# Delta rule's triangular inverse: its transpose is brought forward by products, the inverse is taken from it by TensorE transposes

## The chip, the cores and the metric

The kernel runs on one core of one Trainium2 chip, in one launch. The metric is the device time of that launch in microseconds (us), and lower is better. TensorE (PE) does the matrix products and transposes, VectorE (DVE) and ScalarE (ACT) move results out of PSUM, GpSimd (POOL) does a few small things, and SyncE (SP) issues the transfers.

## The reference, cut to what matters

Two transformer-like blocks run over 1024 tokens of width 1024. The first holds a gated delta rule (4 heads of 128) beside a dilated attention (8 heads of 64), then a projection and a gated feed-forward layer; the second is dense work. Only the delta rule is touched. For each chunk of tokens and each head it solves a unit lower triangular system:

```
lmat = dec_strict * kk * bc[..., None, :]
rhs = jnp.concatenate([vc, gam * kc], axis=-1)
sol = lax.linalg.triangular_solve(lmat, rhs, left_side=True, lower=True, unit_diagonal=True)
u_v, w_k = sol[..., :Dv], sol[..., Dv:]
```

The kernel uses chunks of 128 tokens, so there are 8 chunks, each with four 128x128 systems.

## The kernel before, in words

`gdn_intra` (L881) works on one chunk c for four heads at once; every tile is 128x512, four 128x128 blocks side by side, and each step is a group of four instructions on PE. It forms the strictly triangular matrix LT, and then builds the inverse U and its transpose T by doubling blocks: seven levels, the first of which is elementwise. Two PSUM tiles, pT and pU, hold the running T and U. Each level lv from 1 to 6 does this:

- PE: four products LT x T into a fresh PSUM tile (named ps_G in the profile).
- DVE: this tile times a mask of the level, into G in SBUF.
- PE: four products that add U x G to pT (ps_T), and four that add G x U to pU (ps_pU). At level 6 only pU is needed.
- ACT: copies pT to T and pU to U (at level 6 only U).

Ahead of the loop, pT is filled by four transposes of U, and pU by four transposes of T. After the loop U feeds `w` and the sequential part (`gdn`: ps_u, ps_S from fp32, ps_o). Matrix products of the delta rule are in fp32: the trace shows a weight load and a matmul twice for each product, and once for each transpose. Products run through `mm` (L281), transposes through `tp` (L291) and `tpacc` (L296, which leaves the rest of the PSUM bank as it is), ACT copies through `act` (L311), DVE products through `tt` (L315).

The order of the instructions on each engine is set when the program is built. `Weaver.run` (L137) holds many tasks as Python generators, with estimated costs, picks the next one by estimated readiness and priority, and emits its instructions up to the next `yield`. So the PE queue weaves the chunks' chains with work that does not depend on them: the in-projections of the attention (ps_dil, ps_dv) and, for each attention head, the scores whose maximum is looked for (`dil_scan`: ps_S and ps_S8 from arR, read by DVE). Two neighbouring chunks are in flight at a time: chunk c+1 starts when chunk c has passed level 1 (`ghalf`). `evac` (L343) spawns a copy out of PSUM as a task of its own. When the last scan's maxima are known, they go through DRAM to all heads, and then the attention proper starts (`dil_pv`: ps_T from arR and ps_O). PSUM has eight tiles of 128x512, handed out in turn by `psum` (L357). Engines take their instructions in the order emitted.

Of the kernel before, what the change touches and what calls it, by code (L numbers as in the profile page):

```python
# [73 lines left out]
def after(*evs):  # L74
    def cond():
        return max((e.t for e in evs), default=0.0) if all(e.done for e in evs) else -1.0
    return cond
# [181 lines left out]
class Prog(Weaver):  # L259
# [621 lines left out]
    def gdn_intra(self, c, t):  # L881
        gs = self.gs
        K, Q, V, X, KEM, AT, LT, U, T, GKM = t
        E = KEM
        HH = range(GH)
        for dst, src in ((K, self.kf), (Q, self.qf), (V, self.vf)):
            self.dma(dst, src[:, c * P:(c + 1) * P].rearrange("(h p) t -> p h t", p=P), 262144)
        yield "PE"
        pG = self.ps4("gcb")
        for h in HH:  # L890
            self.tpacc(pG[:, h], gs["gc"][:, c, h:h + 1].to_broadcast([P, P]), h == 0)
        pR = self.ps4("rkb")
        for h in HH:
            self.tp(pR[:, h], gs["rkc"][:, c, h:h + 1].to_broadcast([P, P]))
        pk = self.ps4("kt")
        for h in HH:
            self.tp(pk[:, h], K[:, h])
        pv = self.ps4("vt")
        for h in HH:
            self.tp(pv[:, h], V[:, h])  # L900
        self.tt(X, K, pR, ALU.mult)
        self.act(T, pG, AF.Exp)
        nx = self.ready("PE")
        self.act(V, pv)
        if c:
            for h in HH:
                self.act(GKM[:, h], pk[:, h], AF.Copy, scale=gs["gk"][:, c, h:h + 1])
        self.at = nx
        yield "PE"
        mk = self.maskb  # L910
        for h in HH:
            self.mm(pG[:, h], self.identb, mk, False, True, True)
        pA = self.ps4("A")
        for h in HH:
            self.mm(pA[:, h], K[:, h], Q[:, h], True, True)
        pL = self.ps4("L")
        for h in HH:
            self.mm(pL[:, h], K[:, h], X[:, h], True, True)
        for h in HH:
            self.act(E[:, h], pG[:, h], AF.Exp, bias=gs["ngc"][:, c, h:h + 1])  # L920
        for h in HH:
            self.act(E[:, h], E[:, h], AF.Copy, scale=gs["brk"][:, c, h:h + 1])
        if c:
            self.tt(Q, Q, T, ALU.mult)
        self.tt(LT, pL, E, ALU.mult)
        self.tt(K, LT, self.matb(self.lvl[0]), ALU.mult)
        self.tt(U, self.matb(self.ident), K, ALU.subtract)
        nx = self.ready("PE")
        self.tt(AT, pA, E, ALU.mult)
        for h in HH:  # L930
            self.act(KEM[:, h], pk[:, h], AF.Copy, scale=gs["ke"][:, c, h:h + 1])
        self.at = nx
        yield "PE"
        pT = self.ps4("T")
        for h in HH:
            self.tpacc(pT[:, h], U[:, h], h == 0)
        self.act(T, pT)
        yield "PE"
        pU = self.ps4("pU")
        for h in HH:  # L940
            self.tpacc(pU[:, h], T[:, h], h == 0)
        G = X
        for lv in range(1, 7):
            pG1 = self.ps4("G")
            for h in HH:
                self.mm(pG1[:, h], LT[:, h], T[:, h], True, True)
            self.tt(G, pG1, self.matb(self.lvl[lv]), ALU.mult)
            yield "PE"
            if lv == int(self.STAG):
                self.ghalf[c].set(self.ready())  # L950
            if lv < 6:
                for h in HH:
                    self.mm(pT[:, h], U[:, h], G[:, h], False, True, True)
            for h in HH:
                self.mm(pU[:, h], G[:, h], U[:, h], False, True, True)
            if lv < 6:
                self.act(T, pT)
                nx = self.ready("PE")
                self.act(U, pU)
                self.at = nx  # L960
            else:
                self.act(U, pU)
            yield "PE"
        if c:
            pw = self.ps4("w")
            for h in HH:
                self.mm(pw[:, h], GKM[:, h], U[:, h], True, True)
            self.act(LT, pw)
        self.intra[c] = (Q, AT, KEM, LT, U, V)
# [1146 lines left out]
```

## Time and profile before

| | us |
|---|---|
| median of 3 runs | 2616.55 (2616.05 to 2617.04) |
| the profiled execution, its own time | 2619.11 |
| span of the profiled execution | 2617.3 |
| PE busy | 2540.3 (97%) |
| DVE busy | 1370.7 (52%) |
| ACT busy | 807.9 (31%) |

The span is what the profiler saw from the first to the last instruction. Busy is the union of an engine's instructions, so an engine that is busy all the time has nothing left to hide behind. Matmuls overlap with each other, so the duration of one says less than the distance between the starts of two groups.

### The profile page before, as it was taken

How to read it: one execution, taken by the hardware profiler on the slowest of the kernel's cores; microseconds unless marked ns; L12 is line 12 of the kernel's file. 1: busy time of each engine (PE TensorE's matmuls, PEld its weight loads, DVE VectorE, ACT ScalarE, POOL GpSimd, SP SyncE). 2: the span in 40 equal slices, each digit the busy share in tenths (PEclk: the TensorE clock that was granted, in tenths of full speed). 3: DMA queues.
4: the chain of work that ended last, by engine and by line, in shares of the span. 5: the costliest groups of instructions: out<-in, count | busy, mean ns of one | idle time of the engine just before them, and what ended most of it. 6: DMA issues, size and time to landing. Idle time of an engine off the chain costs nothing.

```text
span 2617.3 us, 31361 instructions
## 1 busy us (share of the span) xinstructions
PE 2540.3 (97%) x13001; PEld 2180.4 (83%) x13001; DVE 1370.7 (52%) x1868; ACT 807.9 (31%) x1306; POOL 121.1 (5%) x245
## 2 busy tenths in 40 slices
PE   7999999988989999999999999989999999999998
PEld 6888999988978888888888888877788888888887
DVE  5441343454654555555555567969554444444444
ACT  5322443453541422222222235253232121212122
POOL 1010000000000000000000001050000000000000
PEclk9999999998989999999999999999999999999999
DMA  5232222232441111111111113102211111111111
GB/s 189 71 104 85 84 67 62 80 80 69 106 130 57 41 49 49 49 50 50 49 50 49 50 66 101 61 9 90 71 41 57 41 57 41 57 41 57 41 49 65
DMA packets 175164, 170.80 MB, mean 65 GB/s; under 512 B 25985, under 2 KB 148254, under 8 KB 175022
## 3 DMA queue, kind: packets, MB, share of 16 engines
q1 hardware_dynamic: 175022, 168.80, 21.2%
q8 instruction: 102, 1.67, 0.3%
q14 instruction: 40, 0.33, 0.0%
HBM read 145.50 MB, written 23.23 MB: 64 GB/s over the span
## 4 chain that ended last, share of the span: by engine, by line
PE 61%; issue 28%; DVE 4%; ACT 3%; DMA 2%; POOL 2%; SPq 0%; POOLq 0%; ACTq 0%; DVEq 0%
PE ps_up L281 18%; PE ps_dn L281 9%; PE ps_in L281 5%; PE ps_out L281 5%; PE ps_vg L281 3%; PE ps_dil L281 3%; PE ps_T L281 2%; ACT arF L311 2%; PE ps_S L281 2%; PE ps_z L281 2%; PE ps_O L281 2%; PE ps_dv L281 2%; DVE arF L327 2%; PE ps_pU L281 1%; PE ps_G L281 1%
## 5 line engine op out<-in xcount | busy, mean ns | idle before, releaser
L281 PE MATMUL ps_up<-arR 128*128 128x512 f32 x3648 | 831.5, 389 | 0.0
L281 PEld LDWEIGHTS ps_up<-arR 128*128 128x128 f32 x3648 | 684.5, 188 | 142.1
L315 DVE TENSOR_TENSOR arR<-arF,arR 128x1024 fp32r<-128x1024 f32 (+3 forms) x283 | 347.6, 1236 | 610.0 <-ACT arR L311 609.5
L281 PE MATMUL ps_dn<-arR 128*128 128x512 f32 x2592 | 591.8, 389 | 0.0
L311 ACT ACTIVATE arR<-arF 128x1024 fp32r<-128x1024 f32 (+3 forms) x297 | 311.2, 1071 | 852.3 <-PE ps_dn L281 394.3
L281 PEld LDWEIGHTS ps_dn<-arR 128*128 128x128 f32 x2592 | 486.4, 188 | 101.0
L315 DVE TENSOR_TENSOR arF<-arF,ps_dn 128x512 f32<-128x512 f32 x416 | 279.6, 684 | 183.2 <-PE ps_dn L281 183.2
L327 DVE SCALAR_TENSOR_TENSOR arF<-arF,pcol 128x1024 f32<-128x1024 f32 (+1 forms) x276 | 311.4, 1149 | 22.5 <-ACT arF L311 17.5
L311 ACT ACTIVATE arF<-arF 128x1024 f32<-128x1024 f32 (+3 forms) x158 | 134.8, 860 | 272.5 <-DVE arF L315 138.5
L281 PE MATMUL ps_out<-arR 128*128 128x512 f32 x768 | 182.2, 398 | 2.7 <-DVE arR L315 2.7
L281 PEld LDWEIGHTS ps_out<-arR 128*128 128x128 f32 x768 | 146.7, 192 | 34.4 <-DVE arR L315 3.7
L311 ACT ACTIVATE arF<-ps_up 128x512 f32<-128x512 f32 x152 | 89.5, 589 | 187.0 <-PE ps_up L281 187.0
L281 PE MATMUL ps_in<-arR 128*128 128x512 f32 x576 | 137.7, 399 | 0.0
L281 PEld LDWEIGHTS ps_in<-arR 128*128 128x128 f32 x576 | 109.4, 192 | 23.9
L315 DVE TENSOR_TENSOR arF<-arF 128x1024 f32<-128x1024 f32 (+4 forms) x91 | 89.1, 979 | 28.8 <-ACT arF L311 14.8
L281 PE MATMUL ps_dil<-arR 128*128 128x512 f32 x384 | 97.4, 403 | 0.0
L281 PE MATMUL ps_vg<-arR 128*128 128x512 f32 x384 | 88.3, 390 | 0.0
L281 PEld LDWEIGHTS ps_vg<-arR 128*128 128x128 f32 x384 | 71.8, 188 | 14.8
L281 PEld LDWEIGHTS ps_dil<-arR 128*128 128x128 f32 x384 | 71.7, 192 | 14.2
L281 PE MATMUL ps_O<-arF 128*128 128x128 f32 (+2 forms) x384 | 69.9, 328 | 12.2 <-ACT arF L311 6.8
L315 DVE TENSOR_TENSOR arF<-ps_G,csq 128x512 f32<-128x512 f32 x48 | 33.1, 690 | 90.8 <-PE ps_G L281 90.8
L315 DVE TENSOR_TENSOR arF<-arF,ps_out 128x512 f32<-128x512 f32 x64 | 43.5, 683 | 62.1 <-PE ps_out L281 62.1
(185 smaller groups left out, 2037.2 us busy)
## 6 DMA issues: line engine op xcount, KB each, us to landing
arF<-in_w_ff_dram SPq DMA_DIRECT2D x64, 512.0 KB
arF<-in_w_up_dram SPq DMA_DIRECT2D x44, 512.0 KB
arF<-in_w_in_dram SPq DMA_DIRECT2D x12, 1024.0 KB
arF<-in_w_down_dram SPq DMA_DIRECT2D x22, 512.0 KB
arF<-in_x_dram SPq DMA_DIRECT2D x16, 512.0 KB
arF<-in_w_out_dram SPq DMA_DIRECT2D x16, 512.0 KB
arF<-in_w_in_dram SPq DMA_DIRECT2D x16, 512.0 KB
arF<-kd SPq DMA_DIRECT2D x28, 256.0 KB
```

Of the source, the lines that this page charges most:

```text
L281: self.nc.tensor.matmul(out, lhsT, rhs, start=start, stop=stop, **kw)
L311: self.nc.scalar.activation(out, in_, func, **kw)
L315: self.nc.vector.tensor_tensor(out, a, b, op)
L327: self.nc.vector.scalar_tensor_tensor(out, a, s, b, op0, op1)
```

## The change

At levels 1 to 5 only T is brought forward by products. pU is no longer held and added to: at each level from 2 to 6, right after the four products of ps_G, four transposes of T go into a fresh PSUM tile (still named ps_pU), and a task of its own on ACT copies them to U. The products that follow wait for this copy as well as for G. At level 6 the last G x U is added to that tile, as before. At level 1, U is still the one made ahead of the loop.

```
-        pU = self.ps4("pU")
-        for h in HH:
-            self.tpacc(pU[:, h], T[:, h], h == 0)
         G = X
         for lv in range(1, 7):
             pG1 = self.ps4("G")
             for h in HH:
                 self.mm(pG1[:, h], LT[:, h], T[:, h], True, True)
+            if lv > 1:
+                pU = self.ps4("pU")
+                for h in HH:
+                    self.tpacc(pU[:, h], T[:, h], h == 0)
+                e = self.evac("ACT", lambda pU=pU: self.act(U, pU), prio=int(self.IP))
             self.tt(G, pG1, self.matb(self.lvl[lv]), ALU.mult)
-            yield "PE"
+            yield "PE", after(e) if lv > 1 else None
             if lv == int(self.STAG):
                 self.ghalf[c].set(self.ready())
             if lv < 6:
                 for h in HH:
                     self.mm(pT[:, h], U[:, h], G[:, h], False, True, True)
-            for h in HH:
-                self.mm(pU[:, h], G[:, h], U[:, h], False, True, True)
-            if lv < 6:
                 self.act(T, pT)
-                nx = self.ready("PE")
-                self.act(U, pU)
-                self.at = nx
             else:
+                for h in HH:
+                    self.mm(pU[:, h], G[:, h], U[:, h], False, True, True)
                 self.act(U, pU)
             yield "PE"
```

The builder's choices change with it, so the order of the woven stretch differs from the first chunk on. Three places show how.

PE in the first chunk, from its first transposes of U (ps_T by L296) on; ps_dil is the attention's in-projection. Before:

```order
L296 MATMUL ps_T<-csq,arF 128x128 x4
L281 MATMUL ps_dil<-arR 128x512 x12
L296 MATMUL ps_pU<-csq,arF 128x128 x4
L281 MATMUL ps_G<-arF 128x128 x4
L281 MATMUL ps_dil<-arR 128x512 x6
L281 MATMUL ps_T<-arF 128x128 x4
L281 MATMUL ps_pU<-arF 128x128 x4
L281 MATMUL ps_dil<-arR 128x512 x6
L281 MATMUL ps_G<-arF 128x128 x4
```

And now:

```order
L296 MATMUL ps_T<-csq,arF 128x128 x4
L281 MATMUL ps_dil<-arR 128x512 x12
L281 MATMUL ps_G<-arF 128x128 x4
L281 MATMUL ps_dil<-arR 128x512 x6
L281 MATMUL ps_T<-arF 128x128 x4
L281 MATMUL ps_dil<-arR 128x512 x6
L281 MATMUL ps_G<-arF 128x128 x4
L296 MATMUL ps_pU<-csq,arF 128x128 x4
L281 MATMUL ps_dil<-arR 128x512 x6
```

The four products into ps_pU are gone from behind ps_T, and four transposes into ps_pU stand behind the second ps_G; independent work still stands between the steps of the chain.

PE in the last two chunks, 6 and 7, with the numbers of the tiles: before, ps_T_4264 is chunk 6 and ps_T_4493 chunk 7, and ps_S and ps_S8 are scores of the last scans.

```order
L296 MATMUL ps_T_4493<-csq_66,arF_69 128x128 x4
L281 MATMUL ps_T_4264<-arF_69 128x128 x4
L281 MATMUL ps_pU_4286<-arF_69 128x128 x4
L296 MATMUL ps_pU_4511<-csq_66,arF_69 128x128 x4
L281 MATMUL ps_G_4516<-arF_69 128x128 x4
L281 MATMUL ps_G_4522<-arF_69 128x128 x4
L281 MATMUL ps_S_4528<-arR_68 128x256 x4
L281 MATMUL ps_T_4493<-arF_69 128x128 x4
L281 MATMUL ps_pU_4511<-arF_69 128x128 x4
L281 MATMUL ps_T_4264<-arF_69 128x128 x4
```

Now ps_T_4389 is chunk 6 and ps_T_4562 chunk 7, ps_L_4526 is chunk 7's product that LT is made from, and ps_mt_4559 is the transpose that ends the last scan:

```order
L281 MATMUL ps_L_4526<-arF_69 128x128 x4
L281 MATMUL ps_G_4548<-arF_69 128x128 x4
L296 MATMUL ps_pU_4553<-csq_66,arF_69 128x128 x4
L291 MATMUL ps_mt_4559<-csq_66,mt_4215 16x128
L296 MATMUL ps_T_4562<-csq_66,arF_69 128x128 x4
L281 MATMUL ps_T_4389<-arF_69 128x128 x4
L281 MATMUL ps_G_4576<-arF_69 128x128 x4
L281 MATMUL ps_G_4582<-arF_69 128x128 x4
L296 MATMUL ps_pU_4587<-csq_66,arF_69 128x128 x4
L281 MATMUL ps_T_4562<-arF_69 128x128 x4
L281 MATMUL ps_G_4606<-arF_69 128x128 x4
L296 MATMUL ps_pU_4611<-csq_66,arF_69 128x128 x4
```

All scans are over before chunk 7's chain begins, and nothing independent is left between its steps: each ps_T is followed at once by the ps_G that reads it. Behind this stretch the attention proper now begins between chunk 7's last steps:

```order
L281 MATMUL ps_T_4562<-arF_69 128x128 x4
L281 MATMUL ps_T_4775<-arR_68 128x256 x4
L281 MATMUL ps_T_4780<-arR_68 128x256 x4
L281 MATMUL ps_T_4787<-arR_68 128x256 x4
L281 MATMUL ps_G_4803<-arF_69 128x128 x4
L296 MATMUL ps_pU_4808<-csq_66,arF_69 128x128 x4
L281 MATMUL ps_O_4685<-arF_69 128x32x4
```

Before, the last ps_o of chunk 7 came first, and the attention's ps_T_4857 and the following stood behind it. From the projection ps_out on, PE's order is the same in both.

## Rows read from the trace of the kernel before

**Rows 1.** The page, busy time by engine (us, share of span, instructions).

```profile
PE 2540.3 (97%) x13001; PEld 2180.4 (83%) x13001; DVE 1370.7 (52%) x1868; ACT 807.9 (31%) x1306; POOL 121.1 (5%) x245
```

**Rows 2.** Stretches: length, busy by engine, PEclk (granted clock), DMA share, GB/s.

```profile
256.00:540.00 284.00, 280.20 (x2092) 267.31 (x2091) 115.25 (x311) 118.89 (x245) 6.01 (x12) 0.99 0.25 73
540.00:652.00 112.00, 90.99 (x669) 87.54 (x668) 53.35 (x151) 53.73 (x104) 8.70 (x16) 0.93 0.33 85
652.00:768.00 116.00, 106.33 (x608) 101.33 (x608) 72.12 (x106) 63.88 (x94) 2.10 (x4) 0.96 0.45 115
```

**Rows 3.** Tile ps_pU on PE: count, minimum/median/maximum ns, first and last start.

```profile
L281 PE MATMUL ps_pU<-arF x384: 270/275/418, 280.0 to 628.9; 128*128 128x128 f32 x192
...
L296 PE MATMUL ps_pU<-csq,arF x32: 270/272/288, 276.4 to 592.8; 128*128 128x128 f32 x32
```

**Rows 4.** Timeline of PE, 276 to 290 us: start, length, operation, count.

```profile
279.08 1.06 PE L281 MATMUL ps_T<-arF 128*128 128x128 f32 x8
279.97 1.06 PE L281 MATMUL ps_pU<-arF 128*128 128x128 f32 x8
...
286.34 0.60 PE L296 MATMUL ps_gcb<-csq,g_gc 128*128 128x128 f32 x4
...
288.09 1.06 PE L281 MATMUL ps_G<-arF 128*128 128x128 f32 x8
```

**Rows 5.** Timeline of all engines, 300 to 320 us: steps of a chain.

```profile
300.68 0.60 PE L296 MATMUL ps_T<-csq,arF 128*128 128x128 f32 x4
...
301.32 0.60 ACT L311 ACTIVATE arF<-ps_T 128x512 f32<-128x512 f32 x1 [1.62 <-PE ps_T L296]
...
302.51 1.06 PE L281 MATMUL ps_T<-arF 128*128 128x128 f32 x8
...
303.61 0.60 ACT L311 ACTIVATE arF<-ps_T 128x512 f32<-128x512 f32 x1 [1.69 <-PE ps_T L281]
...
318.27 1.06 PE L281 MATMUL ps_G<-arF 128*128 128x128 f32 x8
...
319.36 0.69 DVE L315 TENSOR_TENSOR arF<-ps_G,csq 128x512 f32<-128x512 f32 x1 [3.26 <-PE ps_G L281]
```

**Rows 6.** Timeline, 540 to 652 us: PE's waits in brackets, with what ended them.

```profile
551.84 1.13 PE L281 MATMUL ps_pU<-arF 128*128 128x128 f32 x8 [2.37 <-DVE arF L315]
...
553.98 1.06 PE L281 MATMUL ps_L<-arF 128*128 128x128 f32 x8
...
559.00 0.63 PE L296 MATMUL ps_T<-csq,arF 128*128 128x128 f32 x4 [3.07 <-DVE arF L315]
...
574.83 1.12 PE L281 MATMUL ps_S<-arR 128*128 128x128 f32 x4 [2.73 <-DVE arR L315]
...
629.32 0.60 ACT L311 ACTIVATE arF<-ps_pU 128x512 f32<-128x512 f32 x1 [4.17 <-PE ps_pU L281]
629.37 0.28 PE L291 MATMUL ps_mt<-csq,mt 128*16 128x128 f32 x1
...
629.97 1.16 PE L281 MATMUL ps_w<-arF 128*128 128x128 f32 x8 [0.32 <-ACT arF L311]
...
639.14 1.25 PE L291 MATMUL ps_ot<-csq,arF 128*128 128x128 f32 x4 [3.65 <-DVE arF L327]
...
650.04 2.05 PE L281 MATMUL ps_O<-arF 128*128 128x128 f32 x8 [2.58 <-ACT arF L311]
```

**Rows 7.** Timeline of ACT in the same stretch: constants written into new head buffers.

```profile
541.96 3.89 ACT L311 ACTIVATE arR<-csq 64x1024 fp32r<-64x1024 f32 x4
```

**Rows 8.** Short stretches, columns as in rows 2.

```profile
15.00:25.00 10.00, 4.40 (x22) 3.79 (x21) 8.59 (x10) 8.00 (x14) 6.80 (x7) 0.68 0.73 281
548.00:562.00 14.00, 7.85 (x68) 7.22 (x67) 5.31 (x8) 11.04 (x28) 0.00 (x0) 1.00 0.22 50
...
588.00:592.00 4.00, 3.97 (x20) 3.91 (x21) 3.28 (x17) 2.25 (x6) 0.00 (x0) 0.57 0.00 0
```

**Rows 9.** Timeline of PE: four transposes at a lower clock.

```profile
577.45 1.03 PE L296 MATMUL ps_gcb<-csq,g_gc 128*128 128x128 f32 x4
```

## The prediction

> **What bounds the kernel now.** The busy table comes first: PE works in 97% of the span, no other engine in more than 52% [rows 1]. Work taken off PE can thus pay, unless PE then waits where that work stood. So the next view is the stretches of the span around the change [rows 2]. While projections and scores are woven between the chunks (256 to 540 us), PE is busy for 280.20 of 284 us. From 540 to 652 us it is busy for only 90.99 of 112, at a mean clock of 0.93: 21 us idle. In the attention proper, to 768 us, 9.7 us are idle. Behind that the changed program has the same order, and I carry it over unchanged. The timeline of the thin stretch tells why PE waits there [rows 6]: for DVE at the end and at the start of a chunk (2.37 and 3.07 us), for a late attention head (2.73), and, once the delta rule is over, for its output (3.65) and for the transfers that stand between the last scan's transpose at 629.37 and the first ps_O at 650.04.
>
> **PE work removed and added.** ps_pU takes 192 products, each two passes, and 32 transposes, each one pass [rows 3]. Six levels by eight chunks by four heads make 192; five of six levels go, so 160 products, or 40 groups of four. Matmuls overlap, so a group is priced from start to start: the ps_T group starts at 279.08 and the ps_pU group behind it at 279.97, so 0.89 us. Four groups of transposes stand between 286.34 and 288.09, so 0.44 us each [rows 4]. Removed: 40 x 0.89 = 35.6 us. Transposes: 40 groups where there were 8, so 32 more, 14.0 us. Net 21.6 us less on PE. ACT's and DVE's number of instructions is unchanged: 48 copies to U before and now.
>
> The Trainium skill, in "TensorE: Matmul & The Clock Gate", section "Terms", says that the transpose mode is four times faster for fp32. Here it is 0.89 against 0.44, a factor of two, and the measurement decides. By a factor of four a group would cost an estimated 0.22 us, and the net would be 35.6 - 7.0 = 28.6 us.
>
> **Waits the change adds.** Two distances count, and both come from one chain [rows 5]. From the start of ps_T to the start of the ACT copy is 303.61 - 302.51 = 1.10 us, the copy takes 0.60, and the hand-over to PE is 0.05 (a copy ends at 629.92, PE goes on at 629.97 [rows 6]). So the next ps_G can start 1.75 us after ps_T, whose own issue takes 0.89. In the 0.86 us between, PE used to do the ps_pU products, which took 0.89: the wait was covered by the chain itself. Now it needs independent work. The other distance is from ps_G to the next ps_T. By way of G it is 1.09 to the DVE product [rows 5], 0.69 for it, and some 0.15 to PE, 1.93 in all. By way of the new U it is 0.89, then 301.32 - 300.68 = 0.64 from transposes to copy, 0.60 and 0.05, so 2.18: the new copy ends last, by 0.25 us, where nothing else delays either.
>
> I went through the new PE order place by place. Of the 40 places from a ps_T product group to the next ps_G, 33 have projection, scores or the other chunk's work in between that fills the gap. Seven do not: one in the middle, one in chunk 6, and five in the tail of chunks 6 and 7, 7 x 0.86 = 6.0 us. The chain's start in chunk 6 has ps_T by transposes directly before ps_G: 0.64 + 0.60 + 0.05 - 0.44 = 0.85. ps_w stands directly behind chunk 6's last ps_pU: 0.86. Chunk 7's first transposes need DVE's U, which came 559.00 - 553.98 = 5.0 us after the start of ps_L in the chunk before it [rows 6]; between the two now stand only ps_L itself, ps_G, four transposes and ps_mt, 0.89 + 0.89 + 0.44 + 0.1 = 2.3, so PE waits 2.7. On ACT two splits of a head, some 1 us each, are ordered ahead of a copy of T in the tail: 1.0. Sum of the new waits: 11.4 us.
>
> **Waits that go.** Before, 540 to 652 us has 21 us of idle and runs at 0.93, which on 91 us of busy time is 0.07 x 91 = 6.4, so 27 us are lost. What happens to them: the 3.07 at chunk 6's start has four groups of scores in its place now. The 3.65 and the stretch to 650.04 go, since the last scan's transpose now comes before chunk 7's chain, some 30 us before the first ps_O; the transfers that took 20.7 us run beside that chain. The 2.37 stays: ACT still writes constants into the new head buffers between the copies, 3.89 us in one piece [rows 7]. I keep as much again for late heads and for scores that wait for DVE, so 5 us, and 3 us for one fall of the clock. So now 11.4 + 5 + 3 = 19.4 us are lost instead of 27, a gain of 7.6. These come from reading an order, and a wait that I do not see in it can only cost; I take half, 3.8 us. In the attention I keep the 9.7 us.
>
> **The sum.** 21.6 + 3.8 = 25.4 us. The profiled execution took 2619.1 (2.6 more than the median, and 1.8 more than its span); it would be 2593.7. Against the median of 2616.55 I predict **2591 us**. Bounds: if all the 27 us went and only the 11.4 came, the gain would be 21.6 + 15.6 = 37, so 2579. If the new waits were double, or the late heads cost 10 us more, it would be 13, so 2604.
>
> **Rivals.**
>
> *The lost cover decides.* The Weaver fills the gaps by its own estimates; where the filler is late on the chip (ps_S waits for a free PSUM tile, that is for DVE), every step from ps_T to ps_G stays open. All 40 open would cost 40 x 0.86 = 34.4, and the 40 from ps_G to ps_T another 0.25 each, 10, against 21.6 saved: some 23 us slower, 2639. It decides from 25 open places on (21.6 / 0.86). For it: two chunks are all there is in the tail, and idle of 21 us already shows that filler runs out. Against it: up to 540 us PE is idle for only 3.8 us of 284 [rows 2], so filler is there for the first six chunks. Chance 0.06.
>
> *The scans stay late.* PE's queue is in order, and chunk 7's whole chain stands behind the last scan. If the last two heads come no earlier than before (the first waited for at 574.83 [rows 6] hangs on transfers, ACT and DVE, not on PE), the time saved is spent waiting for them, and the chain of some 30 us that used to be woven with their scores follows alone. Each microsecond of delay costs one; I see a margin of about 1 us. Ten late give 2601 to 2604, twenty give about 2612. Chance 0.14 for 2604 to 2611, 0.07 for within 5 us of 2616.
>
> *The clock falls in the tail.* From 15 to 25 us PE runs almost only transposes, is busy for 4.40 of 10 us, and its granted clock is 0.68 of 2.4 GHz on average; from 588 to 592, right after a wait, PE is full at 0.57; 548 to 562, busy 7.85 of 14 us and mostly with products, stays at 1.00 [rows 8]. At the lower level, 1.2 GHz, four transposes last 1.03 us by their row instead of 0.60 [rows 9, 4]. A step of the tail is 1.78 us of products, 0.44 of transposes and 0.86 of waiting, so it is busier than the stretch that kept 1.00, and I expect that here too, but for one fall after the wait of 2.7. Were the tail all at 1.2 GHz, its 24 us of PE work would take 24 more, of which the open waits would absorb some 8: 2591 + 16 = 2607. Chance 0.07. The Trainium skill, in "TensorE: Matmul & The Clock Gate", section "Part 4: PE-mode transpose", says that the full clock does not engage for transposes. The trace agrees only in part: the row from 15 to 25 us has the low clock, but is idle for over half of it, and sixteen transposes in a row from 286.34 kept 0.44 us a group.
>
> That the change does less than it says is excluded by the order: ps_pU has 8 groups of products and 40 of transposes.
>
> **How the numbers follow.** My forecast, 2578 to 2604, has 0.66; the late scans or the clock at 2604 to 2611 have 0.21; no change 0.07; slower by lost cover 0.06. A measurement tells some 0.2% from no change, 5.2 us. Faster thus 0.87, same 0.07, slower 0.06. For 8 in 10 I take 2578 to 2607.
>
> **What would show it.** ps_pU with 64 matmul records by products and 160 by transposes at the same distances, 0.89 and 0.44 us. PE busy lower by about 20 us. In the tail, gaps of 0.8 to 0.9 us ended by ACT between ps_T and ps_G, one of some 2.7 ended by DVE at chunk 7's first ps_T, and a first ps_O some 30 us earlier than 650. No long wait for transfers in front of it. The dense part from ps_out on as long as before. I am wrong if that last part changes, if gaps open before 540 us, or if the first ps_S of the last heads waits long for DVE.

## The result and the profile after

The changed kernel takes 2580.23 us (median of 4 runs, 2579.63 to 2581.34), the kernel before 2616.80 beside it: ratio 0.9859, with a 95% interval of 0.9845 to 0.9873, so some 37 us less (33 to 41). The forecast was 2591, with a range of 2578 to 2607. The profiled execution took 2581.34, with a span of 2579.5, which is 37.8 less than the span before.

The page of the changed kernel, busy time by engine (for [rows 1]):

```profile
PE 2509.1 (97%) x12809; PEld 2149.9 (83%) x12809; DVE 1370.3 (53%) x1868; ACT 803.4 (31%) x1306; POOL 120.6 (5%) x245
```

The tile ps_pU on PE (for [rows 3]): 64 records by products and 160 by transposes, each as long as before. The work removed and added is what was forecast.

```profile
L296 PE MATMUL ps_pU<-csq,arF x160: 272/273/273, 281.5 to 608.5; 128*128 128x128 f32 x160
...
L281 PE MATMUL ps_pU<-arF x64: 270/275/275, 316.9 to 614.6; 128*128 128x128 f32 x64
```

To see where the time went, both spans are cut at the same events: the first ps_O (the attention proper begins), the first ps_out and the first ps_up (the dense part begins). Stretches of the kernel before: length, busy by engine, granted clock, DMA share, GB/s.

```profile
255.00:650.00 395.00, 370.24 (x2754) 353.61 (x2752) 166.60 (x459) 171.62 (x346) 14.71 (x28) 0.98 0.27 76
650.00:768.40 118.40, 108.69 (x617) 103.62 (x617) 74.12 (x109) 66.13 (x97) 2.10 (x4) 0.95 0.46 118
768.40:865.20 96.80, 94.79 (x418) 78.24 (x417) 44.20 (x59) 21.93 (x31) 4.48 (x12) 0.96 0.20 60
865.20:2617.30 1752.10, 1728.49 (x7929) 1439.19 (x7927) 978.52 (x1113) 460.21 (x704) 75.17 (x165) 0.99 0.17 53
```

And of the kernel after:

```profile
255.00:608.60 353.60, 337.67 (x2494) 320.35 (x2493) 162.53 (x444) 165.85 (x341) 9.95 (x20) 0.99 0.29 81
608.60:727.60 119.00, 113.74 (x686) 108.69 (x685) 75.62 (x120) 65.07 (x99) 5.91 (x12) 0.96 0.48 123
727.60:828.50 100.90, 92.78 (x419) 76.68 (x417) 46.29 (x62) 24.74 (x35) 4.48 (x12) 0.97 0.21 63
828.50:2579.50 1751.00, 1726.74 (x7929) 1438.39 (x7927) 978.61 (x1113) 459.62 (x704) 75.62 (x165) 0.99 0.17 53
```

Up to the first ps_O 41.4 us are gained. The attention is as long as before, though 69 more matmuls lie in it: chunk 7's last steps now stand behind the first ps_O (its last ps_pU, ps_w, ps_u and ps_o; two of them are shown), with 12 more of the attention's own ps_T, and the attention's idle time fell from 9.7 to 5.3 us.

```profile
623.17 1.95 PE L281 MATMUL ps_u<-arF 128*128 128x128 f32 x16
...
626.68 1.95 PE L281 MATMUL ps_o<-arF 128*128 128x128 f32 x16
```

Then 4.1 us are lost in ps_out, and the dense part is 1.1 shorter. Sorted by kind, this is 21.6 us of work, as the forecast priced it, and 7.2 us of idle time up to the dense part (24.8 + 9.7 + 2.0 before, 15.9 + 5.3 + 8.1 now). Another 6.3 us is the lower clock: busy time times the clock that is missing, summed over slices of 2 us from 255 us to the dense part, is 16.8 us before and 10.5 now. With the 1.1 that makes 36.2 of 37.8; 1.6 us stay unassigned.

PE in the tail of chunks 6 and 7 after the change: start, length, operation, and in brackets the idle time before it and what ended it.

```profile
568.16 0.27 PE L291 MATMUL ps_mt<-csq,mt 128*16 128x128 f32 x1
570.70 0.82 PE L296 MATMUL ps_T<-csq,arF 128*128 128x128 f32 x4 [2.26 <-DVE arF L315]
573.20 2.08 PE L281 MATMUL ps_T<-arF 128*128 128x128 f32 x8 [1.69 <-ACT arF L311]
575.07 3.27 PE L281 MATMUL ps_G<-arF 128*128 128x128 f32 x16
...
581.84 1.06 PE L281 MATMUL ps_T<-arF 128*128 128x128 f32 x8
583.65 1.16 PE L281 MATMUL ps_G<-arF 128*128 128x128 f32 x8 [0.75 <-ACT arF L311]
...
585.08 1.06 PE L281 MATMUL ps_T<-arF 128*128 128x128 f32 x8
...
608.58 1.07 PE L281 MATMUL ps_O<-arF 128*128 128x128 f32 x8
```

The last scan's ps_mt is over at 568, ahead of chunk 7's chain. A step from ps_T to ps_T takes 585.08 - 581.84 = 3.24 us, of which 0.75 is the open wait for the copy of T. Before, PE was busy for 11.4 of the 20.6 us from the last ps_mt to the first ps_O, at a mean clock of 0.83, so these were not all waiting for transfers, as the prediction has it:

```profile
629.40:650.00 20.60, 11.43 (x69) 10.03 (x69) 6.05 (x13) 5.24 (x10) 2.46 (x5) 0.83 0.73 183
```

Now the chain fills the time between these two events.

### The profile page after: what moved, and what is told of

The parts are those of the page before. It is cut to its first block, busy times and chain, and to the rows that moved or that the text cites. A ratio compares the mean times of both kernels' runs of the same rounds, so it can differ in the third digit from the quotient of the medians.

```text
span 2579.5 us, 30979 instructions
## 1 busy us (share of the span) xinstructions
PE 2509.1 (97%) x12809; PEld 2149.9 (83%) x12809; DVE 1370.3 (53%) x1868; ACT 803.4 (31%) x1306; POOL 120.6 (5%) x245
## 4 chain that ended last, share of the span: by engine, by line
PE 63%; issue 28%; DVE 3%; ACT 3%; POOL 1%; DMA 1%; SPq 0%; POOLq 0%; ACTq 0%; DVEq 0%
PE ps_up L281 19%; PE ps_dn L281 9%; PE ps_out L281 5%; PE ps_in L281 5%; PE ps_vg L281 3%; PE ps_dil L281 3%; PE ps_T L281 3%; PE ps_S L281 2%; PE ps_O L281 2%; PE ps_z L281 2%; PE ps_dv L281 2%; DVE arF L327 2%; ACT arF L311 2%; PE ps_G L281 2%; PE ps_v L281 1%
```

## The experiments

The question was not whether the change pays, but why it paid 11 us more than forecast. Theory W holds that PE's work counts in full. Rival O holds that the new order gives most of it. Times are medians, with the ratio to the kernel before and its 95% interval. Unless a number says otherwise, a difference in us is the ratio times 2616.55.

### Work alone, in the old order

The kernel before, with one edit:

```
             for h in HH:
-                self.mm(pU[:, h], G[:, h], U[:, h], False, True, True)
+                if lv < 6:
+                    self.cost("PE", 213.4)
+                    self.nc.tensor.matmul(pU[:, h], T[:, h], self.ident, start=h == 0, stop=True, is_transpose=True, skip_group_check=True)
+                else:
+                    self.mm(pU[:, h], G[:, h], U[:, h], False, True, True)
```

> The order of the kernel before is kept on every engine, copies and waits included; only the four products into ps_pU of levels 1 to 5 are replaced by four transposes of T into the same places (so U holds a transpose of the old T, and the inverse is not the reference's). Theory W (work): PE bounds the woven stretch, each microsecond of its work is a microsecond: 40 groups x (0.89 - 0.44) = 18 us less, about 2599, and the wait between the last scan's ps_mt and the first ps_O stays at some 20 us. It then follows that the other 18 of the 36.6 us come from the order. Rival O (order): what PE saves is given back as waits for the copies of T, and nearly all of the 36.6 us come from the new order: 2610 to 2617.

Measured: 2598.43 us, ratio 0.9929 (0.9912 to 0.9946), 18.6 us less. That is theory W's number. The wait in front of the attention is still there: ps_mt ends the scan at 613.25, and this is PE behind it.

```profile
623.02 1.25 PE L291 MATMUL ps_ot<-csq,arF 128*128 128x128 f32 x4 [3.65 <-DVE arF L327]
...
626.70 4.43 PE L281 MATMUL ps_T<-arR 97*128 97x256 f32 x23 [2.22 <-DMA arR<-mf]
634.40 1.84 PE L281 MATMUL ps_O<-arF 128*128 128x128 f32 x7 [3.27 <-ACT arF L311]
```

### Order alone, with all the old work

```
-    STEP, SCP, KEEP1, KEEP0, WH = 2, 7, 2, 0, 2
+    STEP, SCP, KEEP1, KEEP0, WH = 2, 3, 2, 0, 2
```

> The kernel before with all its products, and one number of the planner changed: the priority of the scans' scores from 7 to 3, so that the last scan's ps_mt comes before chunk 7's chain, as it does in the changed kernel. If the new order is worth the 15 to 18 us that the work does not explain, this is faster by 10 to 18 us (2599 to 2607), and the first ps_O follows the chain without the 20.7 us of waiting. If the extra came from something else (the clock, fewer instructions), it is within 4 us of the kernel before.

Measured: 2604.80 us, ratio 0.9954 (0.9939 to 0.9969), 12.0 us less (8 to 16), with not one product fewer. PE now goes from the last ps_mt to the first ps_O in 38.6 us of chunk 7's chain, and no wait stands before ps_O:

```profile
592.86 0.27 PE L291 MATMUL ps_mt<-csq,mt 128*16 128x128 f32 x1
...
631.43 1.07 PE L281 MATMUL ps_O<-arF 128*128 128x128 f32 x8
```

The stretches of this kernel show the changed kernel's attention, too: 683 matmuls in the same 118 us.

```profile
255.00:631.40 376.40, 360.20 (x2687) 344.10 (x2686) 162.91 (x445) 169.40 (x340) 11.11 (x20) 0.99 0.27 75
631.40:749.40 118.00, 112.99 (x683) 108.30 (x681) 76.02 (x120) 63.95 (x98) 5.96 (x12) 0.97 0.49 128
```

So this order is worth about a third of the gain, and a planner's number gives it to the kernel before. It brings a loss, too: the first ps_O comes 18.6 us earlier, but ps_out then takes 100.6 us instead of 96.8, as it does in the changed kernel (100.9). And it is not the changed kernel's own order: up to the last ps_mt PE idles for 12.9 of 337.9 us here, for 7.1 of 313 there. What that order is worth is bounded by a run further down, with the products back.

### Both single edits together

The two edits above in one kernel.

> The two single edits together: transposes of T in place of the products of levels 1 to 5 (the inverse is not the reference's), and the scans' priority at 3. If work and order are separate gains, they add: 18.6 + 12.0 = 31 us, 2584 to 2588. If one opens what the other closes (the tail's waits swallow part of the work saved, as the products that cost nothing there suggest), the sum is smaller by 3 to 5 us: 2589 to 2592.

Measured: 2589.02 us, ratio 0.9893 (0.9880 to 0.9907), 28.0 us less (24 to 31). The sum of the two is 30.6, the smaller sum 26 to 28; the interval holds both, so this run doesn't tell them apart. The changed kernel is another 9 us faster. The first eight groups of transposes into ps_pU, which the change drops and this kernel keeps, are 8 x 0.44 = 3.5 of that. The two profiled executions are only 4.1 us apart (spans of 2583.6 and 2579.5), with the first ps_O 5.4 us earlier in the changed kernel (608.6 against 614.0); the rest of the 9 us stays open.

### The products back, in the new order

The changed kernel, with the products of levels 1 to 5 put back beside those into pT:

```
                     self.mm(pT[:, h], U[:, h], G[:, h], False, True, True)
+                for h in HH:
+                    self.nc.tensor.matmul(pG1[:, h], G[:, h], U[:, h], start=True, stop=True)
```

> The changed kernel with 40 groups of four products put back behind the ps_T groups, written into ps_G of the level before and read by nobody (they overwrite values that are already used, so the output does not change); the planner does not count them, so everything else keeps its order. Theory W (work): in chunks 0 to 5 every group costs its 0.89 us, 30 x 0.89 = 26.7; in chunks 6 and 7 a group fills the wait of 0.75 in front of ps_G and costs 0.14 where that wait is open (7 places) and 0.89 in the three others, 3.7: 30 us in all, 2610. Rival O (order): the products lie in waits that the trace does not show as PE's own, and cost less than half of it: 2580 to 2595.

Measured: 2606.73 us, ratio 0.9966 (0.9953 to 0.9979), 26.5 us slower than the changed kernel by the medians. Up to the last ps_mt (568 us in the changed kernel, 594 here) it is 26 us longer, for 32 groups that would be 28.5 by their price. In the tail, eight groups of products, 7.1 us of work, cost only 1.4: 42.0 us instead of 40.6. Its steps there (L957 is the line of the products put back):

```profile
608.07 1.06 PE L281 MATMUL ps_T<-arF 128*128 128x128 f32 x8
608.96 1.06 PE L957 MATMUL ps_G<-arF 128*128 128x128 f32 x8
609.87 1.16 PE L281 MATMUL ps_G<-arF 128*128 128x128 f32 x8
...
611.31 1.06 PE L281 MATMUL ps_T<-arF 128*128 128x128 f32 x8
```

The step is 3.24 us, as without the products: they lie in the 0.75 us of waiting. Where the chain has other work beside it, a product costs nearly its time; where it runs with nothing beside it, it costs next to nothing.

This run also bounds what the changed kernel's own order is worth. It does as many products as the kernel before and 32 groups of transposes more, 14 us by their price, and is still 9 us faster than the kernel before (5 to 12). So that order is worth at least 9 us, and up to 23 if every one of these transposes costs its price. With 23 us for the order, 14 of the 37 us are left for the work, less than the 18.6 that it is worth in the old order. How the gain splits into work and order is no fixed number.

### The order undone in the changed kernel

```
-    DEP, SCANP, SCANO, STAG, GP, CP, CUT = 130.0, 3, 8, 1, 2, 7, 1
+    DEP, SCANP, SCANO, STAG, GP, CP, CUT = 130.0, 3, 0, 1, 2, 7, 1
```

> The changed kernel with one number of the planner changed (the offset of the last scans), so that chunk 7's chain runs alone and the last scan's ps_mt stands behind it again, six groups before the first ps_O. If the order is worth 15 to 18 us, they are lost: 2593 to 2600, with the wait for transfers back in front of the first ps_O. If the gain hangs on the work alone, it stays within 5 us of 2580.

Measured: 2608.69 us, ratio 0.9966 (0.9953 to 0.9979): 28 us lost, more than the 13 to 20 that I expected. Two losses come at once here. The chains of chunks 6 and 7 run with nothing beside them up to 601 us, and the last scores stand between chunk 7's last steps, with the transfers to the attention behind them; PE idles for 32.9 us up to the first ps_O (15.9 in the changed kernel). And chunk 7's last steps stand ahead of the first ps_O again, so that the attention holds 616 matmuls instead of 686 and is hardly shorter for it (117.6 us instead of 119.0):

```profile
616.87 0.28 PE L291 MATMUL ps_mt<-csq,mt 128*16 128x128 f32 x1 [0.87 <-DVE mt L1244]
620.99 1.20 PE L291 MATMUL ps_ot<-csq,arF 128*128 128x128 f32 x4 [3.84 <-issue]
...
628.99 5.25 PE L281 MATMUL ps_T<-arR 97*128 97x256 f32 x23 [6.59 <-DMA arR<-mf]
636.59 2.04 PE L281 MATMUL ps_O<-arF 128*128 128x128 f32 x8 [2.35 <-ACT arF L311]
```

Its time lies among those that I gave for the rival "the scans stay late" (2601 to 2612). But the mechanism is another one: in the rival the scans are late on the chip and chunk 7's chain stands behind them, and here the planner puts the last scores behind most of the chain. So this run does not test the rival. It shows that one planner's number can lose most of the gain.

### Products where the chain is alone

The changed kernel, with the products kept for chunks from HYB on; the first run has HYB = 6, the second 7.

```
+        prod = c >= int(self.HYB)
...
-            if lv > 1:
+            if lv > 1 and not prod:
...
                 for h in HH:
                     self.mm(pT[:, h], U[:, h], G[:, h], False, True, True)
+                if prod:
+                    for h in HH:
+                        self.mm(pU[:, h], G[:, h], U[:, h], False, True, True)
                 self.act(T, pT)
+                if prod:
+                    nx = self.ready("PE")
+                    self.act(U, pU)
+                    self.at = nx
```

> The changed kernel, but chunks 6 and 7, whose chains run with nothing beside them, keep the products of the kernel before; chunks 0 to 5 use the transposes. If the waits of 0.75 us between ps_T and ps_G are the price of the change in the tail, a step there goes from 3.23 us to three product groups, 2.67: five steps give 2.8 us, less 1 to 2 us for products that stand beside other work; 2577 to 2580. If the waits overlap with something else, or the transposes' saving counts there too, it is 1 to 4 us slower than the changed kernel: 2581 to 2584.

Measured: 2577.92 us, ratio 0.9855 (0.9840 to 0.9869). The interval overlaps that of the changed kernel, so the times don't tell the two apart; the trace does, for a step in the tail. From 568 us to the first ps_O it takes 36.2 us instead of 40.6, but 2.5 of these 4.4 us are the clock, which did not fall in this execution and did in another run with the same chain (last section). Two steps in the tail:

```profile
574.18 1.95 PE L282 MATMUL ps_G<-arF 128*128 128x128 f32 x16
576.02 1.16 PE L282 MATMUL ps_T<-arF 128*128 128x128 f32 x8
...
579.70 1.95 PE L282 MATMUL ps_G<-arF 128*128 128x128 f32 x16
```

Two steps, one of each chunk, take 579.70 - 574.18 = 5.52 us, so 2.76 each instead of 3.24, with no wait in them.

> As with products in chunks 6 and 7, but only in chunk 7, whose chain alone runs with nothing beside it. If what counts is the uncovered chain, most of it is chunk 7's five steps: within 2 us of the version with two chunks, 2576 to 2580. If covering the waits of chunk 6 is as important, 2579 to 2581.

Measured: 2588.59 us (2584.81 to 2589.32), ratio 0.9894 (0.9877 to 0.9910): 8 us slower than the changed kernel by the medians, outside both expectations. The tail is no worse (first ps_O at 607.8 instead of 608.6), but this order leaves the attention 122.7 us instead of 119.0, and two of its ps_T wait for the maxima:

```profile
654.17 5.29 PE L282 MATMUL ps_T<-arR 97*128 97x256 f32 x23 [3.40 <-DMA arR<-mf]
684.09 0.60 PE L282 MATMUL ps_T<-arR 97*128 97x256 f32 x3 [1.83 <-DMA arR<-mf]
```

The profiled execution is the fastest of the four, and accounts for 3.5 of the 8 us; the rest stays open. A new order outside the edited stretch can cost more than the edit.

### The new wait in ps_out

In the changed kernel ps_out waits twice, where before it waited once, for 2.01 us:

```profile
727.62 12.62 PE L281 MATMUL ps_out<-arR 128*128 128x512 f32 x54
744.71 0.51 PE L281 MATMUL ps_out<-arR 128*128 128x512 f32 x1 [4.47 <-ACT arR L311]
748.86 70.85 PE L281 MATMUL ps_out<-arR 128*128 128x512 f32 x305 [3.64 <-DVE arR L315]
```

The first wait is for a copy on ACT that had itself waited for a transfer of w_out:

```profile
743.60 4.89 ACT L311 ACTIVATE arR<-arF 128x1024 fp32r<-128x1024 f32 x5 [13.09 <-DMA arF<-in_w_out_dram]
```

SP's own queue there (start, length and operation of each issue) shows the weights standing behind the last head pair's small transfers; a transfer of x now stands between the two into rd:

```profile
727.10 4.29 SPq L339 DMA_DIRECT2D den<-arF  x2
731.48 0.54 SPq L339 DMA_DIRECT2D rd<-den  x1
732.12 0.37 SPq L339 DMA_DIRECT2D arF<-in_x_dram  x1
733.10 0.33 SPq L339 DMA_DIRECT2D rd<-den  x1
737.38 1.12 SPq L339 DMA_DIRECT2D arF<-rd  x2
738.55 12.39 SPq L339 DMA_DIRECT2D arF<-in_w_out_dram  x5
```

The transfers of w_out are issued 10.9 us after ps_out has begun; in the kernel before, 6.1 us after (774.51 against 768.38). One edit moves the first of the five ahead of the two from rd:

```
-            fins.append(self.spawn(self.dil_fin(pr, ob, den, stage, recr), prio=4, eng="SP"))
+            fins.append(self.spawn(self.dil_fin(pr, ob, den, stage, recr), prio=4 if pr else 12, eng="SP"))
```

> The changed kernel with one number changed: the priority of the last head pair's finish is lowered from 4 to 12. The orders of PE and ACT stay the same; on SP's queue one transfer of w_out is issued ahead of the two transfers of rd instead of behind them. If the two waits of 4.47 and 3.64 us inside ps_out (at 744 and 748 us) come from w_out being held behind those transfers on the queue, the first shrinks by 3 to 5 us and the time is 2576 to 2578. If the waits come from the buffers or from the split on ACT and DVE, the time stays within 1.5 us of 2580.

Measured: 2570.40 us, ratio 0.9825 (0.9810 to 0.9839), 9.8 us less than the changed kernel by the medians. The first w_out is issued at 732.33 us, 5.9 after ps_out has begun, and ps_out runs through:

```profile
726.48 82.21 PE L281 MATMUL ps_out<-arR 128*128 128x512 f32 x360
```

I expected only the first of the two waits to shrink. Both went, 8.1 us, and with them the fall of the clock behind them. These are stretches of 4 us of the changed kernel; the granted clock is the first number behind POOL's, 0.88, 0.50 and 0.76:

```profile
742.00:746.00 4.00, 0.51 (x1) 0.19 (x1) 1.84 (x3) 2.40 (x3) 0.00 (x0) 0.88 0.88 333
746.00:750.00 4.00, 1.14 (x3) 0.95 (x4) 4.00 (x5) 2.49 (x3) 0.00 (x0) 0.50 0.01 1
750.00:754.00 4.00, 4.00 (x15) 3.22 (x14) 4.00 (x6) 0.00 (x0) 0.00 (x0) 0.76 0.84 255
```

With the edit it stays at 1.00 there. The lower clock cost 1.6 us in this ps_out stretch, and 8.1 + 1.6 = 9.7. The splits of w_out on DVE come earlier with the transfer, so the edit moves DVE's order as well.

> A control: the kernel before with the same one transfer of w_out moved ahead of the two of rd. If the 9.8 us of that edit belong to the changed kernel alone (there w_out was held up by 4.8 us more than in the kernel before), little is to be had here: 2614 to 2617. If the kernel before lost time by the same queue all along, its ps_out (96.7 us, against 91.0 where nothing waits) gets 5 to 6 us shorter: 2610 to 2612.

The control: 2613.04 us, ratio 0.9986 (0.9977 to 0.9995), 3.7 us less (1 to 6). ps_out goes from 96.8 to 92.4 us. The time lies between my two expectations. So the queue cost the kernel before some 4 us already, and the rest of the 9.8 came with the change's order, 4 to 9 us by the control's interval.

At last both in one kernel, products from chunk 6 on and the transfer moved ahead:

> Chunks 6 and 7 with products and chunks 0 to 5 with transposes, together with the same one transfer of w_out moved ahead. If both gains are separate (2.3 us and 2 to 4 us against the changed kernel), 2574 to 2576; if the moved transfer brings nothing, 2578.

Measured: 2567.89 us, ratio 0.9813 (0.9799 to 0.9828), lower than expected, and the lowest of all kernels: 49 us below the kernel before. Its interval and that of the edit on the transfers alone (2570.40) overlap, so the products in the tail are not shown to add anything in time. Both are faster than the changed kernel, their intervals lying below its own.

## Why the prediction was right, and where it was short

- *PE work, 35.6 removed and 14.0 added*: right. Counts and durations are as forecast, and the work alone, in the old order, is worth 18.6 us for 18.0 by the same prices. By the Trainium skill's figure of a fourfold faster transpose for fp32 ("TensorE: Matmul & The Clock Gate", section "Terms"), taken against a product, that edit would have given an estimated 40 x (0.89 - 0.22) = 26.7 us; its interval ends at 23, so the measurement decides against it once more.
- *Waits the change adds, 11.4 us*: right in sum, 10.2 us by the timeline from 540 us to the first ps_O, which is all of PE's idle time there. Chunk 7's first ps_T waits 2.26 for DVE (2.7 forecast), five ps_G and one ps_w 0.75 (0.86), chunk 6's first ps_G 0.69 (0.85). The 1.0 us on ACT came as 1.69 and for another reason: the copy to U, due at about 568.4, is issued behind a copy of ps_kt on ACT that itself waits 3.15 us for DVE, and starts at 572.53.
- *Waits that go: "I take half, 3.8 us"*: this is the term that was sized wrong, and not by the halving alone. From 540 us to the first ps_O, idle time fell from 21.0 to 10.1 us and what the lower clock costs from 5.6 to 2.6, so 26.6 us were lost before and 12.7 now: a gain of 13.9, where I had 7.6 and kept 3.8. The 5 us that I kept beside the new waits (the 2.37 at a chunk's end, and as much again for late heads and for scores that wait for DVE) did not come at all; the last score now starts at 561.9 us, ahead of chunk 7's chain. The 3 us for the clock came as 2.6. I took half because an order can only be read, not timed; the run with the order alone shows that scans ordered ahead of chunk 7's chain do come early on the chip, and that this is worth 12 us by itself.
- *"In the attention I keep the 9.7 us"*: wrong, in the kernel's favour. The attention lasts 117 to 119.5 us in nine of ten runs and in the changed kernel, with 615 matmuls in it or 687, so chunk 7's last steps, which move behind the first ps_O, are hidden in it. Its idle time fell by 4.4 us and the cost of the lower clock by 0.8. I looked at the first ps_O's time and not at what had moved behind it.
- *"Behind that the changed program has the same order, and I carry it over unchanged"*: true of PE, wrong of the time. SP's order in front of ps_out differs, and ps_out is 4.1 us longer, a sign of being wrong that the prediction itself names. The loss belongs to the new order: the kernel before has it as well when only its scans come early (100.6 us). The rule that every queue is to be followed holds here: I had read PE's.
- *The rivals*: the lost cover did not come, the first part up to 568 us idles for 7.1 of 313 us. The scans did not stay late; no run here makes them late on the chip, so the rival's price is untested. The clock fell in the tail, but only behind the wait at its start: 0.50 to 0.75 from 570 to 578 us, 1.00 from 578 on.

The range held the time because its lower end was worked out from all 27 us going. Between the profiled executions the point is 12.4 us off, 37.8 against 25.4. Counted in idle time and clock as above, 10.1 of it is the waits that go, of which the halving is only 3.8, and 5.2 the attention; against that, 3.7 are lost in ps_out and 1.9 before 540 us. The dense part gives 1.1, and 1.6 stay unassigned. The sum put the attention and ps_out at nothing, and that their errors partly cancel is luck.

## What to carry to other kernels

Work taken off a full engine is worth its price from start to start, but only where other work stands beside it: look for the stretch where the chain runs alone, since there a product may be free and a wait is not. When a change makes a scheduler choose anew, price the new order apart from the work, with a run that has the order alone and one that has the old work in the new order, because a single planner's number may give the order, or take it away, and the two prices need not add up. Follow every queue up to the next stretch that can't be shortened, the small transfers on the issuing engine first.

## What the runs showed of the hardware

- At the start of the tail PE was busy for 1.25 of the 4 us from 568 to 572. It then worked without a gap from 574 to 578 us at 0.50 to 0.54 of its clock; 0.50 is the lower level, 1.2 GHz. The two ps_G groups took 3.10 us from start to start (575.07 to 578.17) instead of 1.78. The two waits there are 2.26 and 1.69 us; the busy time of these slices at their granted clock (0.75, 0.50, 0.50 and 0.54) adds 2.5 to them:

```profile
570.00:572.00 2.00, 0.82 (x4) 0.45 (x4) 1.75 (x3) 0.48 (x2) 0.00 (x0) 0.75 0.00 0
572.00:574.00 2.00, 0.80 (x3) 0.80 (x4) 0.00 (x0) 1.74 (x6) 0.00 (x0) 0.50 0.01 4
574.00:576.00 2.00, 2.00 (x11) 2.00 (x11) 0.00 (x0) 0.60 (x1) 0.00 (x0) 0.50 0.02 5
576.00:578.00 2.00, 2.00 (x12) 2.00 (x12) 0.69 (x1) 0.00 (x0) 0.00 (x0) 0.54 0.03 3
```

- The same waits don't always bring this fall. With products in chunks 6 and 7 the two waits are 2.29 and 0.48 us, and the clock stayed at 1.00. With the same two waits it fell to 0.50 in the run that has these products and the transfer moved ahead (0.78, 0.50 and 0.87 in the slices from 572 to 578 us), and in the run with the order alone (0.86, 0.50 and 0.78 from 596 to 602 us). So products in that place do not keep the clock up by themselves, and two kernels can differ by it alone: the two that share this chain with products take 36.1 and 37.7 us from the last ps_mt to the first ps_O.
- In ps_out 8.1 us of waiting were followed by 0.50 and 0.76, and undoing the waits was worth 9.8 us.
